# Searching one projection at a time, and U products 32 columns narrower, in a hybrid SSD/MLA block with a product-key expert mixer

## The chip, the cores and the metric

The kernel runs on one NeuronCore of a Trainium2 chip. TensorE (PE) multiplies, and its weight loads (PEld) overlap it; VectorE (DVE), ScalarE (ACT) and GpSimd (POOL) work beside it, and transfers are issued by queues of SyncE (SP), POOL and ACT. The metric is the device time of one execution in microseconds, the median of several runs.

## The reference

One decoder layer over 512 tokens of 1024 features, in float32. After a LayerNorm, an SSD part and an attention part are computed and mixed by one output projection, with a residual and a LayerNorm. Neither the change nor the stages it moves touch that part. Then comes the expert mixer:

```python
q = (xb @ w_query).reshape(T, PEER_HEADS, 2, PEER_HALF_DIM)          # 8 heads, 2 halves, 128
s = jnp.einsum('thkd,hknd->thkn', q, sub_keys).astype(jnp.float32)   # 128 sub-keys per half
sv, si = lax.top_k(s, K)                                             # K = 16
cand_s = (sv[:, :, 0, :, None] + sv[:, :, 1, None, :]).reshape(T, PEER_HEADS, K * K)
cand_i = (si[:, :, 0, :, None] * PEER_N_KEYS + si[:, :, 1, None, :]).reshape(T, PEER_HEADS, K * K)
top_s, top_pos = lax.top_k(cand_s, K)
expert_idx = jnp.take_along_axis(cand_i, top_pos, axis=-1)
gate = jax.nn.softmax(top_s, axis=-1)
u = jnp.take(u_table, expert_idx, axis=0)                            # 16384 experts x 1024
act = jax.nn.gelu(jnp.einsum('td,thkd->thk', xb, u).astype(jnp.float32), approximate=False)
v = jnp.take(v_table, expert_idx, axis=0)
return jnp.einsum('thk,thkd->td', (gate * act).astype(xb.dtype), v)
```

So each token chooses 128 of 16384 experts (8 heads x 16). The result gets a residual with factor ALPHA and a last LayerNorm.

## The kernel before, in words

The 512 tokens are four blocks of 128. Every float32 product is made of three products of rounded parts (`mm3`): high x high, high x low and low x high.

For blocks 0 to 2 (NT = 384 tokens) the mixer is dense. All 16384 experts are walked in 128 chunks of 128. A *U product* (`u_chunk`) multiplies a chunk of the U table with the 384 token columns, 8 x 3 matmuls, and ACT puts its GELU into an `act` tile. Gates are written into a dense matrix G: for each token, 128 one-hot pairs are multiplied on PE, so that G holds the gate at each chosen expert and zero elsewhere. A *V product* (`v_chunk`) takes P = act x G, splits it into a high part `Ph` (ACT) and a low part `Pl` (DVE), and multiplies it with a chunk of the V table into six accumulators `va`. Block 3 is not dense: for each of its 128 choices, an indirect DMA on POOL's queue fetches one U row per token, DVE forms the dot products, and later the V rows are added up (`gather`).

All big weights come through one stream (`Stream`, `items`). SP loads a raw tile (`wir`, 3 buffers), ACT rounds it to the high part (`wih`, in one place of four `wihx`), and DVE or POOL subtracts to make the low part (`wil`, line 115; 3 buffers). This subtraction is called a *split* here. A split of item n is issued with the use of item n - 2, waits until item n - 3 has been used, and is followed on SP by the load of a later item. `lo_on` says which engine splits: POOL during the search, DVE otherwise.

The order of the work is written by the program text, and each engine runs its list in order. The stages from about 412 us on:

1. Two U products, then 16 query projections (`w_query_fm`, each 24 matmuls of 512 columns), each followed by the scores of the projection before it against 128 sub-keys (four blocks, in PSUM banks that hold four projections each). Every fourth projection ACT copies the banks to `sc`.
2. The search on DVE (`stage1`, `top16`): for one block and four projections, the top 16 of 128 in two passes of 8, then 88 candidate sums (`cand`) for two heads and their top 16. It starts when four projections are scored.
3. The index stage on DVE (`stage2`): gates, and the expert's two 7-bit indices, block after block. `g_head` transposes the indices and gates of a block on PE.
4. The build (`build_g`): 48 groups of 8 tokens. For a group `hot` makes on DVE the one-hot tiles `oj` and `oi` (two compares) and the two gated tiles `g1` and `oi` (two products), in two buffers each. PE makes 16 fp16 matmuls, ACT copies them to a staging tile `stg`, and every fourth group SP stores 2 MB to a DRAM tensor `gsp`.
5. The second half: U products 54 to 127 alternate with V products 0 on, then V products alone. SP loads `gt` tiles back from `gsp`, which needs the last store. `gather` runs on POOL and DVE beside it.

U products of stages 2 to 4 are placed by a planner in the program text: `tm[0]` sums estimated PE time, `tm[1]` estimated DVE time (the generators yield estimates), and `drive` places a U product (`step_u`) whenever `tm[0] <= tm[1]`, while fewer than LEAD = 54 `act` tiles are filled. Left-over products up to 54 are put behind the build.

Of the kernel before, what the change touches and what calls it, by code (L numbers as in the profile page):

```python
# [11 lines left out]
F32 = mybir.dt.float32  # L12
# [12 lines left out]
D = 1024  # L25
# [5 lines left out]
NT = 384  # L31
LEAD = 54
LASTC = 120
T_U = 4.24
# [5 lines left out]
SCB = 10  # L40
# [9 lines left out]
def tile_block(ctx: ExitStack, tc: tile.TileContext, I, out):  # L50
# [140 lines left out]
    acd = dram.tile([64, 128], F32, name="acd")  # L191

# [676 lines left out]
    XTL = xt.tile([128, 8, S], F32R, name="XTL")  # L869
    lnq = pool("lnq", side="right")  # L870
# [34 lines left out]
    sc, scb, qT = {}, {}, {}  # L905

    def w_query_fm(m):
        if m < 16:
            h, l = item()
            h = h.rearrange("p (k c) -> p k c", k=8)  # L910
            l = l.rearrange("p (k c) -> p k c", k=8)
            ps = pw()
            for k in range(8):
                mm3(ps, h[:, k], l[:, k], XTH[:, k], XTL[:, k], k == 0, k == 7)
            qT[m] = rq.tile([128, S], F32, name="qT", bufs=2)
            A.activation(qT[m], ps, AF.Copy)
        if m > 0:
            m -= 1
            q = qT.pop(m)
            if m % 4 == 0 and m:  # L920
                load_sk(m // 4 + 1)
            for b in range(NB):
                if m % 4 == 0:
                    scb[b] = pu() if b >= 2 else px()
                T.matmul(scb[b][:, (m % 4) * 128:(m % 4 + 1) * 128], q[:, b * 128:(b + 1) * 128], SK[m // 4][:, m % 4],
                         start=True, stop=True)
                if m % 4 == 3:
                    t = rq.tile([128, 4, 128], F32, name="sc", bufs=SCB)
                    A.activation(t.rearrange("p a b -> p (a b)"), scb[b], AF.Copy)  # L929
                    for i in range(4):  # L930
                        sc[b, m - 3 + i] = t[:, i]

    TV, TI, TS, PO = {}, {}, {}, {}

    def top16(src, w, val, idx, gs):
        t2 = {}
        for g in gs:
            V.max(val[:, g, 0:8], src(g))
        for g in gs:
            V.max_index(idx[:, g, 0:8], val[:, g, 0:8], src(g))  # L940
        for g in gs:
            t2[g] = rt.tile([128, 128], F32, name="t2", bufs=4)[:, :w]
            V.match_replace(t2[g], val[:, g, 0:8], src(g), NEG)  # L943
        for g in gs:
            V.max(val[:, g, 8:16], t2[g])
        for g in gs:
            V.max_index(idx[:, g, 8:16], val[:, g, 8:16], t2[g])
        return len(gs) * (0.36 + w * 0.0064)
# [3 lines left out]
    def stage1(b, q):  # L952
        if q == 0:
            TV[b] = rt.tile([128, 16, 16], F32, name="tv", bufs=4)
            TI[b] = rt.tile([128, 16, 16], U32, name="ti", bufs=4)
            TS[b], PO[b] = TS4[:, b], PO4[:, b]
        yield top16(lambda g: sc[b, g], 128, TV[b], TI[b], range(4 * q, 4 * q + 4))
        tv = TV[b].rearrange("p (h e) a -> p h e a", e=2)[:, 2 * q:2 * q + 2]
        cand = rt.tile([128, 2, 88], F32, name="cand", bufs=3)
        for c0, a0, na, w in ((0, 0, 1, 16), (16, 1, 3, 8), (40, 4, 12, 4)):  # L960
            sh = [128, 2, na, w]
            V.tensor_tensor(cand[:, :, c0:c0 + na * w].rearrange("p h (a b) -> p h a b", a=na),
                            tv[:, :, 0, a0:a0 + na, None].to_broadcast(sh),
                            tv[:, :, 1, None, 0:w].to_broadcast(sh), op=OP.add)
        yield 0.5 + top16(lambda g: cand[:, g - 2 * q], 88, TS[b], PO[b], range(2 * q, 2 * q + 2))

    def stage2():
# [35 lines left out]
        for b in range(NB):  # L1003
            for c in range(2):
                A.activation(ti[:, b, :, :, :, c].rearrange("p e h a -> p h e a"),
                             TI[b].rearrange("p (h e) a -> p h e a", e=2), AF.Copy)
            eq = rt2.tile([128, 16, 16, 16], F16, name="eq")
            abv = abf[:, b].rearrange("p e (h k) -> p (e h) k", k=16)
            V.tensor_tensor(eq, abv[:, :, None, :].to_broadcast(sh), iaE[:, None].to_broadcast(sh), op=OP.is_equal)
# [3 lines left out]
            V.tensor_tensor(eqv, eqv, tv[:, :, None, :].to_broadcast([128, 256, 8, 2]), op=OP.mult)  # L1013
# [8 lines left out]
    GT = {}  # L1022

    def g_head(b):
# [4 lines left out]
        ijT = ijp.tile([128, 2, 128], F16, name="ijT", bufs=2)  # L1029
        gT = ijp.tile([128, 2, 128], F16, name="gT", bufs=2)  # L1030
        A.activation(ijT.rearrange("p a b -> p (a b)"), ps[:, 0:256], AF.Copy)
# [4 lines left out]
    def build_g():  # L1036
        bc = [128, 4, 128, 2]

        def hot(n):
# [3 lines left out]
            oj = gb.tile(bc, F16, name="oj", bufs=2)  # L1043
            oi = gb.tile(bc, F16, name="oi", bufs=2)
            g1 = gb.tile(bc, F16, name="g1", bufs=2)
            io = iotaE[:, None].to_broadcast(bc)
            V.tensor_tensor(oj, io, col(ijT[:, 1]), op=OP.is_equal)
            V.tensor_tensor(oi, io, col(ijT[:, 0]), op=OP.is_equal)
# [5 lines left out]
        step_u()  # L1054
        yield 2.7
        for n in range(48):
# [20 lines left out]
            yield 2.7 if n < 47 else 0.1  # L1077
# [39 lines left out]
    ap_ = pool("act")  # L1117
    ACT = {}

    def u_chunk(c, psum=None):  # L1120
# [18 lines left out]
    iaE = ijp.tile([128, 16, 16], F16, name="iaE")  # L1139
    nc.sync.dma_start(iotaE.rearrange("p a b -> p (a b)"), I["ch"][:, 0:256])  # L1140
    nc.sync.dma_start(iaE.rearrange("p a b -> p (a b)"), I["ch"][:, 256:512])
    rt = pool("rt", side="right")
    TS4 = rt.tile([128, NB, 8, 16], F32, name="ts")
    PO4 = rt.tile([128, NB, 8, 16], U32, name="po")
    rq = pool("rq")
# [32 lines left out]
    for m in range(17):  # L1178
        w_query_fm(m)
        tm[0] += T_Q  # L1180
        if m % 4 == 0 and m:
            fill = chain(fill, *[stage1(b, m // 4 - 1) for b in range(NB)])
            tm[1] = max(tm[1], tm[0])
# [7 lines left out]
    close(rq)  # L1191
    rt2 = pool("rt2")
    lo_on[0] = V
# [3 lines left out]
    gb = pool("gb", side="right")  # L1197
    drive(build_g())
# [34 lines left out]
    def v_sb(c, nm):  # L1233
        if c > LASTC:
            return ap_.tile([128, NT], F32, name="act", bufs=LEAD).bitcast(F32R)
# [139 lines left out]
    def ln_out(b):  # L1375
# [4 lines left out]
        for e in range(2):  # L1380
            V.scalar_tensor_tensor(t[:, ce[e]], t[:, ce[e]], ALPHA, va[b][e], op0=OP.mult, op1=OP.add)
# [22 lines left out]

    kept = sorted(held)
# [93 lines left out]
```

## Time and profile before

| | |
|---|---|
| median of 3 runs | 1666.66 us (1665.42 to 1666.8) |
| the profiled execution | 1663.19 us |
| its span | 1661.2 us |
| mean granted PE clock | 0.995 |
| busy: PE, DVE, ACT, POOL | 97%, 82%, 41%, 27% of the span |
| DMA | 384.80 MB, mean 232 GB/s |
| start of the search, index stage, first group on DVE | 455.84, 575.19, 627.29 us |
| last group's DVE work ends, first V product starts | 792.20, 816.18 us |

A row of the order of time has its start, its duration, engine, line and operation, what it writes and reads, the shape, and in brackets how long the engine had been idle and what ended that. Matmul durations overlap, so the pace of PE is read from the starts. A window's row has the stretch, the busy time of PE, PEld, DVE, ACT and POOL with counts, the granted clock, the DMA share and GB/s. L115 is a helper's line (the split).

### The profile page before, as it was taken

To read this page: it belongs to the slowest core of one execution; us is meant where nothing else is said; L and a number is where in the kernel's file an instruction comes from. 1 tells how busy PE (TensorE), PEld (TensorE's weight loads), DVE (VectorE), ACT (ScalarE), POOL (GpSimd) and SP (SyncE) were. 2 spreads that over 40 slices of the span, in tenths; PEclk is the share of its full clock that TensorE was granted. 3 is DMA by queue.
4 is the path that set the end of the run, shared out by engine and by line. 5 is a ranking of instruction groups with operands and counts; after the bars stand their busy time and mean duration, and the time that the engine had idled before them with its cause. 6 is when DMAs were issued, how large, how long until landed. Compare 5 with 4: busy or idle time off the path is not lost.

```text
span 1661.2 us, 23589 instructions
## 1 busy us (share of the span) xinstructions
PE 1618.6 (97%) x8639; PEld 1426.9 (86%) x8639; DVE 1358.3 (82%) x2673; ACT 685.4 (41%) x1082; POOL 449.2 (27%) x315
## 2 busy tenths in 40 slices
PE   7999999999999999999999999999999999999997
PEld 5878777888888998999999999999999999888886
DVE  8979688947299998999487878778788888998977
ACT  5574466632333344555333333333333333333331
POOL 0000000000334400000144555545454544543300
PEclk9999999999999999999999999999999999999999
DMA  6242111463332335666699999999899999999973
GB/s 240 97 151 84 56 54 57 128 237 123 121 98 82 115 125 174 234 237 246 225 364 337 339 319 331 337 333 322 319 342 334 331 320 340 348 344 339 337 227 119
DMA packets 146211, 384.80 MB, mean 232 GB/s; under 512 B 11936, under 2 KB 62368, under 8 KB 144304
## 3 DMA queue, kind: packets, MB, share of 16 engines
q1 hardware_dynamic: 105536, 237.24, 41.4%
q0 software_dynamic: 40416, 145.80, 24.2%
q8 instruction: 67, 1.10, 0.3%
q14 instruction: 48, 0.39, 0.1%
q10 hardware_dynamic: 144, 0.26, 0.0%
HBM read 350.72 MB, written 31.49 MB: 230 GB/s over the span
## 4 chain that ended last, share of the span: by engine, by line
PE 77%; DVE 19%; issue 2%; ACT 1%; DMA 1%; DVEq 0%; SPq 0%; ACTq 0%
PE va L1256 11%; PE va L1257 11%; PE va L1260 11%; PE pu L68 8%; PE pu L70 8%; PE pu L69 8%; PE pa L68 3%; PE pa L70 3%; PE pa L69 3%; DVE wil L115 2%; DVE g L1049 1%; PE pw L69 1%; PE pw L70 1%; PE pw L68 1%; DVE t L943 1%
## 5 line engine op out<-in xcount | busy, mean ns | idle before, releaser
L115 DVE TENSOR_TENSOR wil<-wir,wih 128x1024 fp32r<-128x1024 f32 (+1 forms) x249 | 295.9, 1189 | 116.6 <-issue 59.5
L105 ACT ACTIVATE wih<-wir 128x1024 fp32r<-128x1024 f32 (+2 forms) x269 | 277.7, 1033 | 220.5 <-DMA wir<-v 85.0
L70 PE MATMUL pu<-XTH,wil 128*128 128x384 f32 x1008 | 341.9, 339 | 0.0
L68 PE MATMUL pu<-XTH,wih 128*128 128x384 f32 x904 | 309.2, 342 | 1.0 <-ACT sc L929 1.0
L69 PE MATMUL pu<-XTL,wih 128*128 128x384 f32 x904 | 306.5, 339 | 0.0
L1293 POOL DMA_INDIRECT row<-u,ix x128 | 187.1, 1462 | 425.9 <-DVE g L1278 252.3
L1257 PE MATMUL va<-wil,Ph 128*128 128x512 f32 x726 | 283.6, 391 | 0.0
L1293 POOL DMA_INDIRECT row<-v,ix x128 | 182.3, 1424 | 204.3 <-DVE ac L1310 174.5
L1128 ACT ACTIVATE act<-pu 128x384 f32<-128x384 f32 x126 | 61.9, 491 | 317.4 <-PE pu L70 317.3
L70 PEld LDWEIGHTS pu<-XTH,wil 128*128 128x128 f32 x1008 | 189.7, 188 | 0.0
L68 PEld LDWEIGHTS pu<-XTH,wih 128*128 128x128 f32 x904 | 170.3, 188 | 4.0 <-ACT sc L929 1.2
L69 PEld LDWEIGHTS pu<-XTL,wih 128*128 128x128 f32 x904 | 170.5, 189 | 2.8
L1256 PE MATMUL va<-wih,Ph 128*128 128x512 f32 x432 | 168.5, 390 | 0.0
L1310 DVE SCALAR_TENSOR_TENSOR ac<-row,hd,ac 128x1024 f32<-128x1024 f32 x128 | 164.0, 1281 | 2.7 <-DMA row<-v,ix 0.5
L1257 PEld LDWEIGHTS va<-wil,Ph 128*128 128x128 f32 x726 | 136.2, 188 | 26.4
L1304 DVE SCALAR_TENSOR_TENSOR row<-row,x 128x1024 f32<-128x1024 f32 x128 | 150.0, 1219 | 2.1 <-DMA row<-u,ix 2.0
L1260 PE MATMUL va<-wih,Pl 128*128 128x512 f32 x432 | 133.3, 390 | 0.0
L105 ACT ACTIVATE wihx<-wir 128x1024 fp32r<-128x1024 f32 x67 | 71.2, 1063 | 145.2 <-DMA wir<-v 101.2
L115 DVE TENSOR_TENSOR wil<-wir,wihx 128x1024 fp32r<-128x1024 f32 x61 | 74.6, 1222 | 60.5 <-issue 55.5
L1256 PE MATMUL va<-wihx,Ph 128*128 128x512 f32 x294 | 115.0, 391 | 1.5 <-ACT Ph L1240 1.5
L115 POOL TENSOR_TENSOR wil<-wir,wih 128x1024 fp32r<-128x1024 f32 x20 | 49.5, 2474 | 193.7 <-PE pw L70 165.8
L1260 PEld LDWEIGHTS va<-wih,Pl 128*128 128x128 f32 x432 | 81.1, 188 | 16.9
(435 smaller groups left out, 3062.9 us busy)
## 6 DMA issues: line engine op xcount, KB each, us to landing
wir<-ut SPq DMA_DIRECT2D x128, 512.0 KB, 5.2
wir<-v SPq DMA_DIRECT2D x128, 512.0 KB, 6.4
gsp<-stg SPq DMA_DIRECT2D x12, 2048.0 KB, 7.2
gt<-gsp SPq DMA_DIRECT2D x32, 768.0 KB, 10.0
wir<-wo SPq DMA_DIRECT2D x26, 512.0 KB, 3.8
wir<-wf SPq DMA_DIRECT2D x18, 512.0 KB, 3.3
wir<-wqr SPq DMA_DIRECT2D x16, 512.0 KB, 3.6
de<-acd POOLq DMA_DIRECT2D x8, 512.0 KB, 5.2
```

What stands on the lines that cost most here:

```text
L68: T.matmul(ps, lh, rh, start=start, stop=False)
L69: T.matmul(ps, lh, rl, start=False, stop=False)
L70: T.matmul(ps, ll, rh, start=False, stop=stop)
L105: A.activation(h, r, AF.Copy)
L115: self.lo(n).tensor_tensor(l, r, h, op=OP.subtract)
L1128: A.activation(ACT[c], ps, AF.Gelu)
L1256: T.matmul(va[b][e], Ph[:, bs], h[:, cs], start=c == 0, stop=False)
L1257: T.matmul(va[b][e], Ph[:, bs], l[:, cs], start=False, stop=False)
L1260: T.matmul(va[b][e], Pl[:, bs], h[:, cs], start=False, stop=c == 127)
L1293: G.indirect_dma_start(out=R[s], out_offset=None, in_=I["u"] if s < 128 else I["v"], in_offset=bass.IndirectOffsetOnAxis(ap=ix[:, s % 128: ...
L1304: V.scalar_tensor_tensor(r, r, 1.0, x3, op0=OP.mult, op1=OP.mult, accum_out=hd[:, s:s + 1])
L1310: V.scalar_tensor_tensor(ac, r, hd[:, s - 128:s - 127], ac, op0=OP.mult, op1=OP.add)
```

## The change

**The search goes projection by projection.** The scores of a projection now stand inside the next one, after its third of eight k steps, in one PSUM bank for all four blocks, and are copied out at once. `stage1(m)` searches one projection for four blocks; after every second one come the candidates of one head for four blocks. `TV4` and `TI4` hold the results of all blocks.

**U products have 352 columns.** NU = NT - 32: the last 32 tokens of block 2 are left out of the products. Their 32 columns of each `act` tile are filled with ones (`one`, an ACT copy).

**These 32 tokens get their activations by gathering.** The index stage takes block 2 first, and `ug_index` writes their 32 x 128 expert indices to DRAM and reads them back with 4 choices x 32 tokens on the 128 partitions, on POOL's queue; the gates go the same way. 32 indirect DMAs (`ug_fetch`, two buffers) each fetch 128 U rows, and in build groups 1 to 32 DVE makes one dot product each (`ug_dots`), followed by a GELU and another trip over DRAM. `ug_head`, after group 41, multiplies activation and gate, scales each token by its largest magnitude, transposes, and puts the product into the gate tile of block 2. Since `act` is one there, P is right; `scl` multiplies the scale back in the last addition of block 2 (`ln_out`), whose residual ACT has multiplied by ALPHA before.

**The build.** The two compares of a group are one, over both indices (`ij`); `ijT` is laid out for that.

**The planner.** T_U is 3.9, a group 2.55. The row buffers lie where 8 of the 54 `act` tiles go (`KEEP = 46`): until the dots are done and the pool `ug` is closed, only 46 U products may be placed. In the engines' lists as they come out, PE has 21 U products between the last projection and the first group, 23 one by one between the first groups, none between groups 23 and 33, eight in a row behind group 33, and none between the last 14 groups; one stands before the first V product. DVE has the eight splits of that row ahead of the compare of group 35. 21 splits are POOL's (before: 26). The table `iaE` is loaded later, into `rt2`.

```diff
@@ scores inside the next projection
+        for k in range(8):
+            if m < 16:
                 mm3(ps, h[:, k], l[:, k], XTH[:, k], XTL[:, k], k == 0, k == 7)
+            if k == 2 and m > 0:
+                sub_scores(m - 1)
...
+    def sub_scores(m):
+        q = qT.pop(m)
+        if m % 4 == 0 and m:
+            load_sk(m // 4 + 1)
+        ps = px()
+        for b in range(NB):
+            bs = slice(b * 128, (b + 1) * 128)
+            T.matmul(ps[:, bs], q[:, bs], SK[m // 4][:, m % 4], start=True, stop=True)
+        sc[m] = rq.tile([128, NB, 128], F32, name="sc", bufs=SCB)
+        A.activation(sc[m].rearrange("p a b -> p (a b)"), ps, AF.Copy)
...
+    def stage1(m):
+        yield top16(sc.pop(m), 128, TV4[:, :, m], TI4[:, :, m])
+        if m % 2:
+            h = m // 2
...
+            yield 0.7 + top16(cand, 88, TS4[:, :, h], PO4[:, :, h])
@@ index stage
-        for b in range(NB):
+        for b in (2, 0, 1, 3):
...
             if b == 2:
+                ug_index(p3)
+            if b == 1:
                 g_head(0)
@@ gathered vectors
+    def ug_fetch(n):
+        if n < UG:
+            UR[n] = ug.tile([128, D], F32, name="urow", bufs=2)
+            G.indirect_dma_start(out=UR[n], out_offset=None, in_=I["u"],
+                                 in_offset=bass.IndirectOffsetOnAxis(ap=UR["ix"][:, n:n + 1], axis=0))
+
+    def ug_dots():
+        for n in range(UG):
+            r = UR.pop(n)
+            V.scalar_tensor_tensor(r, r, 1.0, UR["x"], op0=OP.mult, op1=OP.mult, accum_out=UR["hd"][:, n:n + 1])
+            ug_fetch(n + 2)
+            yield 1.2
...
+        close(ug)
+        aps.append(pool("act2"))
+        yield 0.1
+
+    def ug_head():
+        w, g = UR["w"], UR["g"]
+        mx, r = UR["m"][:, 0:1], UR["m"][:, 1:2]
+        V.tensor_tensor(w, w, g, op=OP.mult)
+        V.scalar_tensor_tensor(g, w, -1.0, w, op0=OP.mult, op1=OP.max)
+        V.tensor_reduce(mx, g, axis=AX.X, op=OP.max)
...
+        T.transpose(ps[:, :UG], w, ident[:UG, :UG])
...
@@ build
-            V.tensor_tensor(oj, io, col(ijT[:, 1]), op=OP.is_equal)
-            V.tensor_tensor(oi, io, col(ijT[:, 0]), op=OP.is_equal)
+            V.tensor_tensor(ij.rearrange("p e q i c -> p (e q) i c"), iotaE[:, None].to_broadcast(b2),
+                            ijT[:, n % 16].rearrange("p e (q c) -> p (e q) c", c=2)[:, :, None, :].to_broadcast(b2),
+                            op=OP.is_equal)
+            oi, oj = ij[:, 0], ij[:, 1]
...
+            if n >= 1:
+                tm[1] += next(dots, 0.0)
+            if n == 41:
+                ug_head()
+                tm[1] += 1.2
-            yield 2.7 if n < 47 else 0.1
+            yield 2.55 if n < 47 else 0.1
@@ U products
-        ps = (psum or pu)()[:, :NT]
+        ps = (psum or pu)()[:, :NU]
         for k in range(8):
-            mm3(ps, h[:, k], l[:, k], XTH[:, k, :NT], XTL[:, k, :NT], k == 0, k == 7)
-        ACT[c] = ap_.tile([128, NT], F32, name="act", bufs=LEAD)
-        A.activation(ACT[c], ps, AF.Gelu)
+            mm3(ps, h[:, k], l[:, k], XTH[:, k, :NU], XTL[:, k, :NU], k == 0, k == 7)
+        ACT[c] = act_tile()
+        A.activation(ACT[c][:, NU:], one, AF.Copy)
+        A.activation(ACT[c][:, :NU], ps, AF.Gelu)
@@ planner
-            if tm[0] <= tm[1] and un[0] < LEAD:
+            if tm[0] <= tm[1] and un[0] < (LEAD if len(aps) > 1 else KEEP):
@@ last addition
+            if b == 2:
+                V.scalar_tensor_tensor(t[:, ce[e]], va[b][e], scl, t[:, ce[e]], op0=OP.mult, op1=OP.add)
...
+    A.activation(xr[2], xr[2], AF.Copy, scale=ALPHA)
```

More of the change, by code (lines that the diff above doesn't have):

```diff
@@ L31 @@
 NT = 384
+UG = 32
+NU = NT - UG
 LEAD = 54
+KEEP = 46
 LASTC = 120
-T_U = 4.24
+T_U = 3.9
 T_Q = 6.3
@@ new lines, in top16 @@
+    def top16(src, w, val, idx):
+        t2 = []
+        for b in range(NB):
+            V.max(val[:, b, 0:8], src[:, b])
+        for b in range(NB):
+            V.max_index(idx[:, b, 0:8], val[:, b, 0:8], src[:, b])
+        for b in range(NB):
+            t2.append(rt.tile([128, 128], F32, name="t2", bufs=4)[:, :w])
+            V.match_replace(t2[b], val[:, b, 0:8], src[:, b], NEG)
+        for b in range(NB):
+            V.max(val[:, b, 8:16], t2[b])
+        for b in range(NB):
+            V.max_index(idx[:, b, 8:16], val[:, b, 8:16], t2[b])
+        return NB * (0.36 + w * 0.0064)
@@ L1053, in build_g @@
         nxt = hot(0)
-        step_u()
-        yield 2.7
+        dots = ug_dots()
+        tm[1] += 3.0
+        yield 2.6
         for n in range(48):
@@ L1180, in tile_block @@
         tm[0] += T_Q
-        if m % 4 == 0 and m:
-            fill = chain(fill, *[stage1(b, m // 4 - 1) for b in range(NB)])
-            tm[1] = max(tm[1], tm[0])
+        if m:
+            fill = chain(fill, stage1(m - 1))
+            tm[1] = max(tm[1], tm[0] - 3.0)
         while tm[1] < tm[0] + T_Q:
```

127 lines of the change are left out of this document (68 added, 59 removed).

## The prediction

> **What bounds the kernel now.** I read the page first, then stages of 100 us, then the order of time on TensorE (PE) and VectorE (DVE) from the search to the second half.
>
> ```profile
> PE 1618.6 (97%) x8639; PEld 1426.9 (86%) x8639; DVE 1358.3 (82%) x2673; ACT 685.4 (41%) x1082; POOL 449.2 (27%) x315
> ...
> PE 77%; DVE 19%; issue 2%; ACT 1%; DMA 1%; DVEq 0%; SPq 0%; ACTq 0%
> ```
>
> The chain that ended last is PE with a fifth of DVE. The stages tell where that fifth lies (columns: stretch, busy time by engine, granted clock, DMA share, GB/s).
>
> ```profile
> 600.00:700.00 100.00, 94.12 (x727) 91.14 (x726) 93.01 (x120) 49.52 (x83) 0.00 (x0) 0.97 0.52 179
> 900.00:1000.00 100.00, 100.00 (x504) 91.12 (x503) 79.83 (x118) 35.17 (x48) 52.67 (x35) 1.00 0.94 327
> 1400.00:1500.00 100.00, 100.00 (x460) 85.17 (x459) 87.91 (x101) 36.00 (x49) 48.71 (x33) 1.00 0.97 343
> ```
>
> From about 816 us on (U and V products) PE never stops; DVE is the pace from the search (456 us) to the end of the build (792 us), with PE filled by U products beside it.
>
> **What a narrower U product is worth.** Starts of a U product, of the V product behind it, and of 256-wide products:
>
> ```profile
> 1004.36 0.34 PE L68 MATMUL pu<-XTH,wih 128*128 128x384 f32 x1
> 1008.60 0.40 PE L1256 MATMUL va<-wih,Ph 128*128 128x512 f32 x1
> ...
> 214.34 0.28 PE L69 MATMUL pu<-wil,kvh 128*128 128x256 f32 x1
> 215.53 0.28 PE L70 MATMUL pu<-wih,kvl 128*128 128x256 f32 x1
> ```
>
> 24 matmuls take 4.24 us, 0.1767 us each. Ten 256-wide ones start within 1.19 us, 0.119 each. On the line between, 352 columns cost 0.1623 us: 3.894 us a product, 0.346 less. 55 of the 128 products lie before the first V product, 73 behind it. There nothing hides PE, so 73 x 0.346 = **25.3 us** go. The new 32-wide ACT copy per product lies on an engine busy 35 of 100 us there: nothing; without that cover, 128 short copies.
>
> **The search starts earlier.**
>
> ```profile
> 423.08 0.49 PE L68 MATMUL pw<-XTH,wih 128*128 128x512 f32 x1 [0.25 <-ACT XTH L902]
> 434.98 0.60 PE L925 MATMUL px<-SK,qT 128*128 128x128 f32 x4
> 441.47 0.61 PE L925 MATMUL px<-SK,qT 128*128 128x128 f32 x4
> ...
> 455.84 0.87 DVE L938 MAX8 tv<-sc 128x8 f32<-128x128 f32 x4 [31.39 <-ACT sc L929]
> 462.97 0.85 DVE L938 MAX8 tv<-sc 128x8 f32<-128x128 f32 x4
> 467.64 0.46 DVE L962 TENSOR_TENSOR cand<-tv 128x32 f32<-128x32 f32 x3
> 470.07 0.85 DVE L938 MAX8 tv<-sc 128x8 f32<-128x128 f32 x4
> 575.19 0.67 DVE L972 TENSOR_TENSOR dd<-ts 128x512 f32<-128x512 f32 x1
> ```
>
> Now DVE waits 31 us for four score groups, 6.49 us apart. After the change the first scores stand 9 matmuls into the second projection. Projections begin 0.6 us earlier (two narrower U products), at 422.5; one projection with its start is about 6.3 us, nine matmuls 2.1: scores at 430.9, and, with 1.8 us for four products and the copy out, search from 432.7. One score group costs 467.64 - 462.97 = 4.67 us; the candidates of two heads 470.07 - 467.64 = 2.43, of four blocks about 4.45 (the additions rise less than twofold). 16 x 4.67 + 8 x 4.45 = 110.3; 1.8 us of waiting for the second group; today's 119.35 us exceeds 16 x 7.10 by 5.7 (bounds 0 to 5.7), of which I keep 2.6. The search ends at **547.4**, 27.8 us earlier.
>
> **Index stage and build.**
>
> ```profile
> 586.69 2.28 DVE L1009 TENSOR_TENSOR eq<-abf,iaE 128x4096 f16<-128x4096 f16 x1
> 588.89 1.21 DVE L115 TENSOR_TENSOR wil<-wir,wih 128x1024 fp32r<-128x1024 f32 x1
> 590.03 2.28 DVE L1013 TENSOR_TENSOR eq<-eq,tif 128x4096 f16<-128x4096 f16 x1
> ...
> 627.29 0.69 DVE L1047 TENSOR_TENSOR oj<-iotaE,ijT 128x1024 f16<-128x1024 f16 x1
> 633.74 0.68 DVE L1047 TENSOR_TENSOR oj<-iotaE,ijT 128x1024 f16<-128x1024 f16 x1
> 634.35 0.68 DVE L1048 TENSOR_TENSOR oi<-iotaE,ijT 128x1024 f16<-128x1024 f16 x1
> 635.06 0.69 DVE L1049 TENSOR_TENSOR g<-oi,gT 128x1024 f16<-128x1024 f16 x1
> 636.40 0.68 DVE L1047 TENSOR_TENSOR oj<-iotaE,ijT 128x1024 f16<-128x1024 f16 x1
> ...
> 1002.78 1.22 DVE L1304 SCALAR_TENSOR_TENSOR row<-row,x 128x1024 f32<-128x1024 f32 x1
> 1003.93 1.22 DVE L1304 SCALAR_TENSOR_TENSOR row<-row,x 128x1024 f32<-128x1024 f32 x1
> ```
>
> The index stage took 627.29 - 575.19 = 52.1 us. One more split of a weight (590.03 - 588.89 = 1.14), the index arithmetic (0.3) and a wait for the PE transposes of the first block, now late (1.6), make 55.1: first group's DVE work at 602.5. The x rows and the small table queue on SP behind loads that U products of the search need, not ahead of them; the index round trip over DRAM is on POOL's queue with some 35 us to spare: nothing.
>
> A group costs DVE 2.66 us. Its two compares (1.32) become one of twice the size: between 0.61 and 2.20 for 1024 and 4096 elements lies 1.14, plus the 0.1 of a dependent successor, 1.25; a group 2.59 (bounds 2.45 to 2.7). A dot with a gathered row adds 1.15, a split 1.14. The group of PE:
>
> ```profile
> 778.16 0.23 PE L1067 MATMUL pw<-oi,oj 128*128 128x128 f16 x1
> 779.98 0.42 PE L68 MATMUL pu<-XTH,wih 128*128 128x384 f32 x1
> 784.30 0.23 PE L1067 MATMUL pw<-oi,oj 128*128 128x128 f16 x1
> ...
> 802.05 1.23 DVE L115 TENSOR_TENSOR wil<-wir,wih 128x1024 fp32r<-128x1024 f32 x1 [3.02 <-PE pu L70]
> ```
>
> Two groups take 1.82 us, 0.91 each; a narrower product there 4.32 - 0.35 = 3.97. So group and product cost PE 4.88 and group, dot and split cost DVE 4.88. Projections end at 527, 21 products and the transposes at 609.2; with DVE's third group this meets at 613. Then, in DVE's new order, 32 groups with a dot, 22 of them with a split: 32 x 3.74 + 22 x 1.14 = 144.8; 1 for two gate tiles; 2 for the coupling (the build's 164.9 us from 627.29 to 792.2 hold 6.7 beyond its 48 x 2.66, 26 splits and gate tiles, so 0 to 6.7); and 3 for rows that land late (below). DVE is done with group 34 at **763.8**. In the last ten of these PE has 0.91 us of work in 3.74: the limit of 46 products holds it idle.
>
> Then eight products stand in a row on PE, and eight splits on DVE ahead of group 35. The row at 802.05 shows what a split does there: three buffers, so it waits until the product three places back is through. DVE is held for the whole run. PE begins it after group 33, 761.8, runs 8 x 3.89 + 2.5 (clock), and is through at 795.4, group 34 at 796.3. Twelve groups at 2.59 without any product beside them and 3 us for the gathered gates (six small operations, a transpose, a copy; 1.5 to 6) end at **830.4**.
>
> **The hand-over.**
>
> ```profile
> 792.20 1.22 DVE L115 TENSOR_TENSOR wil<-wir,wih 128x1024 fp32r<-128x1024 f32 x1
> ...
> 794.12 0.33 SPq L1074 DMA_DIRECT2D gsp<-stg  x1
> 808.31 1.35 SPq L1215 DMA_DIRECT2D gt<-gsp  x2
> ...
> gsp<-stg SPq DMA_DIRECT2D x1, 2048.0 KB, 7.3
> ...
> 814.97 0.56 DVE L1227 TENSOR_TENSOR P<-act,gt 128x384 f32<-128x384 f32 x1 [7.45 <-DMA gt<-gsp]
> ...
> 816.18 0.51 PE L1256 MATMUL va<-wihx,Ph 128*128 128x512 f32 x1 [1.51 <-ACT Ph L1240]
> ```
>
> 1.9 us to the store's issue, 7.3 to land, 6.7 for the load back (today issued late, behind weight loads on SP's queue), 1.2 to the first V product: 17.1. Five U products cover it today; one is left. First V product at 847.5 against 816.18: **+31.3**, and 2 for a cold clock.
>
> ```profile
> 636.00:637.00 1.00, 0.46 (x5) 0.50 0.00 0
> ```
>
> The clock fell to 0.50 here after two gaps of 1.6 us with 0.9 us of work between; half speed for up to 5.9 us would cost 0 to 2.95 in either place. I take 2.5 and 2. The Trainium skill (TensorE: Matmul & The Clock Gate, What's actually happening) has the clock halve only after an idle window of about 3.4 us. By that rule the gaps before the run of eight would not halve it, and the sum would be 2.5 us lower; this case's row disagrees, and the row decides.
>
> **Sum:** 31.3 + 2 - 25.3 = +8.0 us. The scaled last addition and one early ACT copy change nothing at the end. The profiled execution took 1663.19 us, 1671.2 after; the median is 3.5 above it: **1674.7**. Differences under 0.2% (3.3 us) cannot be told from none.
>
> **Rivals.**
>
> Not slower: the hand-over is short. These are the GB/s from 785 to 810 us, in 40 slices.
>
> ```profile
> GB/s 419 210 210 85 360 360 59 0 7 301 360 164 7 0 0 210 472 393 367 498 446 446 157 367 33 269 413 420 419 125 52 321 354 138 0 0 0 72 111 295
> ```
>
> Single slices reach 446 and more. With empty queues the store's 2 MB may land in 4.6 us and the load in half of 6.7. Price 6.1, time 1668.6; it decides from 4.7. Against it: today's store had little beside it.
>
> The group is cheaper: a fused compare that cost no more than one of today (0.71 with its successor's wait) takes 0.54 from the 21 groups with no product beside them, 11.3 us: 1663.4, faster if it is less still. Against it: compares grow with their size in the rows above.
>
> Warm clock: PE's gaps before the run of eight are 3.74 - 0.91 = 2.8 us; if they do not slow it, 2.5 us less, 1672.2.
>
> Late rows: only two row buffers. A row must land within two groups less a dot and a hand-shake (1.35): 8.4 us with products, 6.1 without.
>
> ```profile
> DMA to landing us min/median/max: 5.6/8.5/11.0
> ```
>
> At 8.5 the ten groups without products lose 12 us, 9 more than I took: 1684; at 11 all 32 lose, over 50. [...]
>
> Memory is the limit in the second half: 327 GB/s must become 341 for the whole gain. The stage at 343 with PE full speaks against it; half the gain lost is 1687. And the change may not do what it says: a matmul that does not get shorter below 384 columns gives 44 us back, about 1719; the 256-wide rows speak against it.
>
> **Chances.** Forecast 0.46; short hand-over 0.15; warm clock 0.08; cheap group or a build otherwise shorter 0.13; late rows 0.10; memory 0.06; width 0.02. Cheap group makes faster, 0.13; short hand-over and 0.02 of the forecast's low end the same, 0.17; the rest, 0.70, slower. The range takes 1660 to 1688; the forecast's own is 1670 to 1682.
>
> **What would show it.** Search from about 433 to 547 us; 0.162 us between 352-wide matmuls; group 35's compare some 25 us behind its predecessor with splits waiting on PE between; thirteen groups with PE mostly idle; first V product 27 to 35 us later than now; from there to the end about 25 us less. Wrong, if the first V product comes by 841 us, or dots wait for rows, or PE waits in the second half.

## The result, and the profile after

The changed kernel takes 1685.8 us (median of four runs, 1685.18 to 1688.45), the kernel before 1666.34 in the runs beside it (1665.42 to 1666.8). The ratio is 1.012, interval 1.0104 to 1.0135: 19.5 us slower, where 8 were forecast. The profiled execution took 1685.18 us, its span is 1683.4.

The page of the changed kernel, busy times and the chain that ended last:

```profile
PE 1594.6 (95%) x8640; PEld 1399.9 (83%) x8640; DVE 1397.7 (83%) x2680; ACT 704.0 (42%) x1213; POOL 495.5 (29%) x349
...
PE 81%; DVE 8%; issue 6%; POOL 2%; DMA 2%; ACT 2%; DVEq 0%; POOLq 0%; ACTq 0%; SPq 0%
```

TensorE (PE) does 24 us less work than before, and VectorE (DVE) 39 more. POOL is new on the chain with 2%, and DMA's share of it goes from 1% to 2%. The stages, in the columns of the prediction's second fence:

```profile
600.00:700.00 100.00, 94.51 (x739) 92.13 (x738) 89.68 (x110) 49.94 (x95) 25.22 (x15) 0.97 0.71 250
700.00:800.00 100.00, 74.41 (x562) 70.81 (x562) 77.79 (x99) 38.57 (x73) 26.56 (x17) 0.78 0.68 245
800.00:900.00 100.00, 78.95 (x507) 71.55 (x507) 65.34 (x89) 36.13 (x64) 17.54 (x13) 0.78 0.64 230
900.00:1000.00 100.00, 100.00 (x528) 90.61 (x527) 83.70 (x124) 37.98 (x62) 53.32 (x36) 1.00 0.97 352
1400.00:1500.00 100.00, 100.00 (x486) 86.75 (x485) 89.71 (x97) 38.07 (x57) 51.61 (x35) 1.00 0.99 358
```

From 900 us on PE is full, as before, and the DMA engines deliver 352 and 358 GB/s where they delivered 327 and 343. From 700 to 900 us PE and DVE are both idle for a fifth to a third of the time: neither is the limit there, waits between them are. DVE's instructions give the milestones (columns: start, duration, engine and line, tiles; in brackets the idle time ahead and what ended it):

```profile
437.30 0.87 DVE L946 MAX8 tv<-sc 128x8 f32<-128x128 f32 x4 [10.14 <-ACT sc L941]
552.83 0.67 DVE L977 TENSOR_TENSOR dd<-ts 128x512 f32<-128x512 f32 x1
607.16 1.22 DVE L1102 TENSOR_TENSOR ij<-iotaE,ijT 128x2048 f16<-128x2048 f16 x1
...
782.37 1.23 DVE L1052 SCALAR_TENSOR_TENSOR urow<-urow,ux 128x1024 f32<-128x1024 f32 x1 [3.48 <-DMA urow<-u,uix]
...
783.52 1.22 DVE L1102 TENSOR_TENSOR ij<-iotaE,ijT 128x2048 f16<-128x2048 f16 x1
...
802.01 1.23 DVE L118 TENSOR_TENSOR wil<-wir,wih 128x1024 fp32r<-128x1024 f32 x1 [2.61 <-PE pu L73]
...
810.83 1.22 DVE L1102 TENSOR_TENSOR ij<-iotaE,ijT 128x2048 f16<-128x2048 f16 x1
...
814.41 1.23 DVE L1102 TENSOR_TENSOR ij<-iotaE,ijT 128x2048 f16<-128x2048 f16 x1 [0.91 <-PE pw L1126]
817.00 1.22 DVE L1102 TENSOR_TENSOR ij<-iotaE,ijT 128x2048 f16<-128x2048 f16 x1
...
845.18 1.22 DVE L1102 TENSOR_TENSOR ij<-iotaE,ijT 128x2048 f16<-128x2048 f16 x1
...
862.70 0.56 DVE L1308 TENSOR_TENSOR P<-act,gt 128x384 f32<-128x384 f32 x1 [14.85 <-DMA gt<-gsp]
```

The search runs from 437.30 to 552.83, the first group starts at 607.16. The last dot starts at 782.37, the compare of group 34 (groups are counted from 0) 1.15 us later at 783.52, so that group is done at 783.52 + 2.59 = 786.1. Then the splits of the row of eight products wait for PE, up to the compare of group 35 at 810.83; that of group 36, at 814.41, waits 0.91 us more for PE. From there groups follow each other in 2.59; the last ends at 845.18 + 2.59 = 847.8. The first V product is this row of PE:

```profile
863.87 0.80 PE L1337 MATMUL va<-wihx,Ph 128*128 128x512 f32 x1 [8.64 <-ACT Ph L1321]
```

| stretch, us | forecast | measured | difference |
|---|---|---|---|
| start to search | 432.7 | 437.3 | +4.6 |
| search | 114.7 | 115.5 | +0.8 |
| index stage, to the first group | 55.1 | 54.3 | -0.8 |
| first group to group 34 done | 161.3 | 178.9 | **+17.6** |
| from there to the last group | 66.6 | 61.7 | -4.9 |
| hand-over, to the first V product | 17.1 | 16.1 | -1.0 |
| first V product to the end of the span | 821.7 | 819.5 | -2.2 |

The differences add up to 14.1, and 1685.18 - 1671.2 is 14.0. One stretch holds more than all of it, the groups with dots. The 4.9 us that come back behind it belong to it for the larger part: while the last dot waited 3.48 us for its row, PE had already begun the row of eight (at 780.59, which is 5.5 us before group 34 was done; the forecast had 2.0). The group of the dots in the list of costly instructions, its busy time and mean, and the idle time ahead of it with its releaser:

```profile
L1052 DVE SCALAR_TENSOR_TENSOR urow<-urow,ux 128x1024 f32<-128x1024 f32 x32 | 39.0, 1220 | 22.2 <-DMA urow<-u,uix 22.2
```

DVE waited 22.2 us for gathered rows; the forecast had 3. There are eight waits. Three of them, then SP's stores of finished blocks in the same stretch:

```profile
639.94 1.23 DVE L1052 SCALAR_TENSOR_TENSOR urow<-urow,ux 128x1024 f32<-128x1024 f32 x1 [2.06 <-DMA urow<-u,uix]
661.27 1.23 DVE L1052 SCALAR_TENSOR_TENSOR urow<-urow,ux 128x1024 f32<-128x1024 f32 x1 [1.75 <-DMA urow<-u,uix]
680.21 1.22 DVE L1052 SCALAR_TENSOR_TENSOR urow<-urow,ux 128x1024 f32<-128x1024 f32 x1 [5.18 <-DMA urow<-u,uix]
```

```profile
630.09 0.33 SPq L1132 DMA_DIRECT2D gsp<-stg  x1
649.43 0.33 SPq L1132 DMA_DIRECT2D gsp<-stg  x1
668.92 0.42 SPq L1132 DMA_DIRECT2D gsp<-stg  x1
```

Each of the eight comes about ten microseconds behind the issue of a 2 MB store (639.94 behind 630.09, 661.27 behind 649.43, 680.21 behind 668.92), once in a block of four groups. That raises the question for the experiments: do rows come late because of the store, or are two buffers too few for what a fetch takes anyway, or is GpSimd (POOL) held up when it issues the fetches?

### The profile page after: what moved, and what is told of

It reads as the page before. It is cut to its first block, busy times and chain, and to the rows that moved or that the text cites. A ratio compares the mean times of both kernels' runs of the same rounds, so it can differ in the third digit from the quotient of the medians.

```text
span 1683.4 us, 23810 instructions
## 1 busy us (share of the span) xinstructions
PE 1594.6 (95%) x8640; PEld 1399.9 (83%) x8640; DVE 1397.7 (83%) x2680; ACT 704.0 (42%) x1213; POOL 495.5 (29%) x349
## 4 chain that ended last, share of the span: by engine, by line
PE 81%; DVE 8%; issue 6%; POOL 2%; DMA 2%; ACT 2%; DVEq 0%; POOLq 0%; ACTq 0%; SPq 0%
PE va L1337 10%; PE va L1338 10%; PE va L1341 10%; PE pu L71 9%; PE pu L72 9%; PE pu L73 9%; PE pa L73 3%; PE pa L72 3%; PE pa L71 3%; PE pw L72 3%; PE pw L73 3%; PE pw L71 3%; POOL urow L1046 2%; DVE ij L1102 1%; PE pb L490 1%
## 5 line engine op out<-in xcount | busy, mean ns | idle before, releaser
L118 DVE TENSOR_TENSOR wil<-wir,wih 128x1024 fp32r<-128x1024 f32 (+1 forms) x253 | 300.9, 1190 | 109.3 <-ACT wih L108 58.9
L73 PE MATMUL pu<-XTH,wil 128*128 128x352 f32 x1008 | 327.4, 325 | 0.0
L71 PE MATMUL pu<-XTH,wih 128*128 128x352 f32 x904 | 296.5, 328 | 0.0
L72 PE MATMUL pu<-XTL,wih 128*128 128x352 f32 x904 | 294.6, 326 | 0.0
L1198 ACT ACTIVATE act<-pu 128x352 f32<-128x352 f32 x126 | 58.4, 464 | 188.6 <-PE pu L73 188.4
L118 DVE TENSOR_TENSOR wil<-wir,wihx 128x1024 fp32r<-128x1024 f32 x62 | 78.0, 1259 | 43.0 <-issue 32.7
L1125 PE MATMUL pw<-ij 128*128 128x128 f16 x384 | 64.6, 256 | 41.3 <-DVE ij L1107 41.3
```

Source lines behind the costliest of these rows:

```text
L71: T.matmul(ps, lh, rh, start=start, stop=False)
L72: T.matmul(ps, lh, rl, start=False, stop=False)
L73: T.matmul(ps, ll, rh, start=False, stop=stop)
L118: self.lo(n).tensor_tensor(l, r, h, op=OP.subtract)
L1125: T.matmul(ps[:, t * 128:(t + 1) * 128], oj[:, q, :, c], oi[:, q, :, c], start=True, stop=False)
```

## Experiments

### What makes the rows late: the store twice, and in quarters

```
             if g % 4 == 3:
                 nc.sync.dma_start(gsp[b * 4 + g // 4], stg)
+                if n < 32:
+                    nc.sync.dma_start(gs2[b * 4 + g // 4], stg)
```

> Each of the first eight stores of the build is issued twice, the second time to another place in memory; nothing reads the copy. Theory A (rows queue behind stores): the waits for rows about double, 35 to 55 us, the time 1698 to 1720. Theory B (latency or GpSimd): waits stay near 22 us, the time within 4 us of 1686. If the staging buffers come free too late, ACT waits for them, which would show as a wait on stg and not on urow.

```
+        full = []
...
-            if g % 4 == 3:
-                nc.sync.dma_start(gsp[b * 4 + g // 4], stg)
+            if g % 4 == 3:
+                full.append((b * 4 + g // 4, stg))
+            k, s4 = full[-1] if full else (0, None)
+            if n == 47:
+                nc.sync.dma_start(gsp[k], s4)
+            elif n >= 3:
+                cs4 = slice((n + 1) % 4 * 32, (n + 1) % 4 * 32 + 32)
+                nc.sync.dma_start(gsp[k][:, cs4], s4[:, cs4])
```

> The 2 MB store of a finished block of the build is cut into four stores of 512 KB, one behind each of the next four groups; the last block's goes out whole. Theory A (a gathered row queues behind the store's packets on the shared DMA engines): the 22.2 us that dots wait for rows fall under 10, group 34 comes 12 to 18 us earlier, the time is 1668 to 1674. Theory B (two row buffers are too few for the plain latency, or GpSimd is kept from writing descriptors): the waits stay at 18 to 26 us, the time within 4 us of 1686.

The store twice: 1702.2 us (ratio 1.0209, interval 1.0192 to 1.0226). The store in quarters: 1674.5 us (1.0047, 1.0030 to 1.0064). Dots and fetches of the doubled store, of the changed kernel, and of the quarters (the same view of three kernels; the dot's row of the changed kernel stands above):

```profile
L1047 POOL DMA_INDIRECT urow<-u,uix x32 | 53.6, 1675 | 156.5 <-DVE urow L1053 153.4 <-DMA uix<-ugi 2.8 <-issue 0.3
L1053 DVE SCALAR_TENSOR_TENSOR urow<-urow,ux 128x1024 f32<-128x1024 f32 x32 | 39.1, 1221 | 41.6 <-DMA urow<-u,uix 41.6
```

```profile
L1046 POOL DMA_INDIRECT urow<-u,uix x32 | 53.4, 1669 | 139.7 <-DVE urow L1052 136.4 <-DMA uix<-ugi 3.0 <-issue 0.3
```

```profile
L1046 POOL DMA_INDIRECT urow<-u,uix x32 | 53.5, 1672 | 130.5 <-DVE urow L1052 127.4 <-DMA uix<-ugi 2.8 <-issue 0.3
L1052 DVE SCALAR_TENSOR_TENSOR urow<-urow,ux 128x1024 f32<-128x1024 f32 x32 | 39.1, 1222 | 10.1 <-DMA urow<-u,uix 10.1
```

The waits go 41.6, 22.2, 10.1 us with nothing changed but the stores, and the times follow them. Against the kernel before, timed beside each, the three take 35.0, 19.5 and 7.3 us more: +15.6 and -12.2 us, where +19.4 and -12.1 us of waiting were added and taken. (The quarters are at the edge of what theory A gave, 10.1 us for "under 10" and 1674.5 for 1668 to 1674.) In the doubled run ACT never waits for a staging buffer. What POOL spends on a fetch stays at 1.67 to 1.68 us in all three, so whatever POOL meets there is no cause of the differences. Theory B falls as the cause of these differences: it is the store that makes the rows late. The 10.1 us that are left with quarters, in 16 short waits, no run explains. How the store does it (rows behind its packets, as theory A has it, or both waiting on memory) these runs do not tell. The Trainium skill (DMA: Bandwidth & Descriptors, Issuing engines are not separate DMA queues) says that transfers started by SP and by GpSimd run on the same DMA engines and interleave; the three waits (41.6, 22.2 and 10.1 us) agree with it.

### What the waits cost: three row buffers

```
-KEEP = 46
+KEEP = 43
...
-            UR[n] = ug.tile([128, D], F32, name="urow", bufs=2)
+            UR[n] = ug.tile([128, D], F32, name="urow", bufs=3)
...
-            ug_fetch(n + 2)
+            ug_fetch(n + 3)
```

> Three buffers for gathered rows instead of two, each row fetched three groups ahead; for their space eleven products instead of eight are held back to the end of the dots. By both theories on the rows (behind stores, or latency) the waits fall from 22.2 to 0 to 5 us: this prices them. Against it three more products in the row, 3 x 3.9 us of PE behind the dots, less 3 splits of 1.14 ahead: +8. Time 1686 - 20 + 8 = 1674, range 1669 to 1680. If the waits were covered by something else, 1690 to 1694.

Measured 1671.7 us (1.0029, 1.0019 to 1.0038), within the range. No dot waited:

```profile
L1052 DVE SCALAR_TENSOR_TENSOR urow<-urow,ux 128x1024 f32<-128x1024 f32 x32 | 38.9, 1217 | 0.0
```

Of the 22.2 us some 14 reach the time (1685.8 less 1671.7). The rest goes against the row of products, now eleven long, and against the 3.48 us that the last dot had waited beside it. The stretch to the end of the dots, which no longer waits on anything but DVE, is also a clean look at the clock: PE's longest gap there is 2.64 us, and from 713 us on the gaps are 1.20 to 2.64 us. Two starts of a group on PE, and then stages of this kernel:

```profile
717.13 0.29 PE L1125 MATMUL pw<-ij 128*128 128x128 f16 x1 [2.64 <-DVE ij L1107]
720.86 0.29 PE L1125 MATMUL pw<-ij 128*128 128x128 f16 x1 [1.85 <-DVE ij L1107]
```

```profile
710.00:715.00 5.00, 2.10 (x33) 1.75 (x32) 4.93 (x7) 2.48 (x5) 1.81 (x2) 0.96 0.98 389
715.00:720.00 5.00, 1.89 (x16) 1.62 (x16) 4.90 (x7) 1.34 (x3) 2.94 (x2) 0.50 0.56 199
...
750.00:755.00 5.00, 2.23 (x20) 1.98 (x21) 4.90 (x8) 1.19 (x2) 0.00 (x0) 0.50 0.98 416
```

The granted clock falls to 0.50 with such gaps and stays there for 40 us.

### The row of eight products

```
-            if tm[0] <= tm[1] and un[0] < (LEAD if len(aps) > 1 else KEEP):
+            if tm[0] <= tm[1] and un[0] < KEEP + rel[0]:
...
+            if n in (35, 38, 41, 44):
+                rel[0] += 1
```

> The eight U products held back until the dots are through no longer stand in a row: one is let go behind each of groups 35, 38, 41 and 44, and four stand behind the last group. Theory C (the row holds DVE, as its splits wait for buffers, and the hand-over is uncovered): from group 34's end at 786 us the rest takes 13 x 2.59 + 4 x 1.2 + 2.3 = 41 us, last group at 827 instead of 847.8; the hand-over then takes 16 to 22 us, as the load queues behind weights on SP; first V product at 843 to 849 instead of 863.9, the time 1665 to 1671. Rival (PE has this work to do in any case and only moves it): within 4 us of 1686.

Measured 1677.1 us (1.0052, 1.0034 to 1.0069): theory C is right in sign, 8.7 us instead of 15 to 21. DVE after the dots (rows of DVE in order of time):

```profile
796.76 1.23 DVE L1102 TENSOR_TENSOR ij<-iotaE,ijT 128x2048 f16<-128x2048 f16 x1 [2.42 <-PE pw L1126]
...
820.90 1.22 DVE L1102 TENSOR_TENSOR ij<-iotaE,ijT 128x2048 f16<-128x2048 f16 x1 [2.60 <-PE pw L1126]
...
831.14 1.23 DVE L1102 TENSOR_TENSOR ij<-iotaE,ijT 128x2048 f16<-128x2048 f16 x1 [1.26 <-PE pw L1126]
...
856.30 0.56 DVE L1311 TENSOR_TENSOR P<-act,gt 128x384 f32<-128x384 f32 x1 [6.89 <-DMA gt<-gsp]
```

Two things ate the rest. A product of 3.9 us on PE between groups of 2.59 on DVE holds back the group behind it, so that a compare waits 1.26 to 2.6 us (the compares' buffers are two), and the last group ends at 831.14 + 2.59 = 833.7, not 827. And with four weight loads ahead of it on SP's queue the gate load is late: from there to the first V product (857.52) it is 23.8 us, where the changed kernel took 16.1. So the last group comes 14 of the forecast 21 us earlier, and the later hand-over takes 8 of these back. The rival's number (within 4 us of 1686) does not hold either; that part of the row was PE work which has to be done in any case fits the result, but no run separates it.

### The width alone

```
-        ps = (psum or pu)()[:, :NT]
+        ps = (psum or pu)()[:, :NU]
...
-        A.activation(ACT[c], ps, AF.Gelu)
+        A.activation(ACT[c][:, NU:], one, AF.Copy)
+        A.activation(ACT[c][:, :NU], ps, AF.Gelu)
```

> The kernel before with nothing changed but the width: U products 352 columns wide, and ones in the place of the 32 other inputs, whose vectors are left out of the computation. My term: 73 x 0.346 = 25.3 us less from the first V product to the end. Ahead of it DVE is the pace, but PE stood at 93 to 98% there: 0 to 13 us more. Time 1628 to 1641. If memory limits the second half: half of it, 1652 to 1656 and a DMA rate that stays near 340 GB/s with PE waiting.

Measured 1635.1 us (0.9806, 0.9789 to 0.9822). Its span is 1634.3, and its first V product is this:

```profile
816.52 0.50 PE L1260 MATMUL va<-wihx,Ph 128*128 128x512 f32 x1 [2.03 <-ACT Ph L1244]
```

So from the first V product to the end it takes 817.8 us, 27.2 less than before (forecast 25.3). The first V product itself comes no earlier (816.52 against 816.18), although PE had less to do ahead of it. One reason may be the start of the search: it is 4.6 us later in this run (460.47 against 455.84; see the late start below), and no run has the width alone without that. In this order of the work the narrower products bring 27 us, and the gather has to be cheaper.

### The search without the gather

```
-UG = 32
-NU = NT - UG
+NU = NT
...
-KEEP = 46
+KEEP = LEAD
...
-T_U = 3.9
+T_U = 3.7
```

and all that has `ug` or `UR` in its name taken out.

> The change without the gather: search by projection and the fused compare stay, U products are 384 wide, no rows, no dots, no held products, the end as before; 3.7 us planned for a product, so that five are left behind the last group as in the kernel before. If DVE alone were the limit, the search (20 us) and the 48 groups (0.07 us each) would bring the first V product to about 793 and the time to 1643. Theory: PE stood idle for only 11 of the 396 us from 420 to 816 in the kernel before, so no more than that can go: first V product at 806 to 814, time 1656 to 1664. If the search gives nothing, 1667.

Measured 1654.8 us (0.9929, 0.9911 to 0.9946), 1.2 us below the range; the first V product, at 806.61, is within it. The stretch from 420 to 816 us of the kernel before and of this one:

```profile
420.00:816.00 396.00, 384.83 (x2581) 359.04 (x2579) 333.84 (x1102) 169.27 (x269) 64.03 (x26) 0.99 0.48 166
```

```profile
420.00:816.00 396.00, 390.32 (x2626) 363.93 (x2626) 340.95 (x1047) 174.41 (x276) 57.06 (x24) 1.00 0.50 169
```

PE was busy for 384.8 of 396 us already, so a search that ends 26 us earlier on DVE (549.01 against 575.19) brings the first V product 9.6 us forward and no more. This part of the change is a gain by itself. The gather, with the row of held products and the hand-over left uncovered, turns it into a loss: the first V product comes at 863.87 instead of 806.61, 57 us later, of which the narrower products give 25.5 back, and some 31 remain between the two kernels.

### The late start of the search

Ahead of the search, DVE's splits and the one of POOL in the changed kernel:

```profile
421.45 1.22 DVE L118 TENSOR_TENSOR wil<-wir,wih 128x1024 fp32r<-128x1024 f32 x1
422.59 3.38 DVE L118 TENSOR_TENSOR wil<-wir,wihx 128x1024 fp32r<-128x1024 f32 x1
425.89 1.27 DVE L913 TENSOR_TENSOR XTL<-px,XTH 128x512 fp32r<-128x512 f32 x2
```

```profile
421.87 3.01 POOL L118 TENSOR_TENSOR wil<-wir,wih 128x1024 fp32r<-128x1024 f32 x1 [128.14 <-PE pw L73]
```

In the kernel before, the same two splits began in the other order:

```profile
422.03 1.22 DVE L115 TENSOR_TENSOR wil<-wir,wihx 128x1024 fp32r<-128x1024 f32 x1
```

```profile
422.10 3.40 POOL L115 TENSOR_TENSOR wil<-wir,wih 128x1024 fp32r<-128x1024 f32 x1 [129.60 <-PE pw L70]
```

A split of this size takes 1.22 us on DVE and, begun 0.72 us behind a split on POOL, 3.38. The order goes with the width of the products ahead: in the run with the width alone DVE's split takes 3.37 us, in the run without the gather, at full width, 1.22. Two runs tried to part them; the first asks for POOL's split one projection later, the second gives it to DVE.

```
     lo_on[0] = G
+    win.la = 1
...
         w_query_fm(m)
+        win.la = 2
```

> GpSimd's first split of a query weight is asked for one projection later, so that it cannot run beside VectorE's split ahead of the last XTL. If the two engines keep each other out there (VectorE's split 3.38 us instead of 1.22, TensorE idle and its clock lowered behind it), the split takes 1.22, the search starts at 433 to 434 instead of 437.3 and the time is 1681 to 1683. If the late start is TensorE's own, the search starts at 437 as before and the time stays at 1686.

```
-    lo_on[0] = G
...
         w_query_fm(m)
+        lo_on[0] = G
```

> VectorE instead of GpSimd does the split of a query weight that ran beside the split ahead of the last XTL. Here the two cannot meet: the split ahead of XTL should take 1.22 us instead of 3.38, and the span from its start to the first score search should fall from 14.7 us (422.59 to 437.30) to 12.5; the time from 1685 to about 1683. If the 3.38 us are not from the meeting, both stay. A change of 2 us of the time can hardly be told; the durations can.

The first gave 1683.7 us (1.0093, 1.0074 to 1.0113) and tests nothing: POOL has no other work there, so its split started (420.26) 0.73 us ahead of DVE's as before, and DVE's took 3.38 us again. The second, 1680.2 us (1.0100, 1.0071 to 1.0129), parts them; here are its rows of DVE:

```profile
421.19 1.22 DVE L118 TENSOR_TENSOR wil<-wir,wihx 128x1024 fp32r<-128x1024 f32 x1
...
432.35 0.88 DVE L946 MAX8 tv<-sc 128x8 f32<-128x128 f32 x4 [7.61 <-ACT sc L941]
```

The split takes 1.22 us, and from its start to the first search it is 11.2 us instead of 14.7: 3.5 us of the late start go with this meeting. In the time the difference cannot be told apart (the intervals overlap). The Trainium skill (SBUF — State Buffer, SBUF: two separate sides) describes a pair of ports that GpSimd shares with DVE: a DVE operation with two SBUF inputs and a GpSimd operation that reads SBUF exclude each other, and whoever starts first has the pair for the whole instruction. The trace agrees: POOL's split in the changed kernel ends at 421.87 + 3.01 = 424.88, and 1.1 us later DVE's is through.

### All repairs, and half the gather

Three row buffers, stores in quarters, the edit of the first split run, the products let go one by one, and two gate loads issued ahead of the weights of the last four, with 32 gathered inputs:

```
+            if n in (33, 34, 36, 38, 40, 42, 44):
+                rel[0] += 1
...
+    close(gb)
+    gtp = pool("gtp")
+    load_g(0)
+    load_g(1)
     uc = un[0]
     while uc < LEAD:
```

> All repairs together: stores in quarters, three row buffers, GpSimd's first split one projection later, held products let go one by one (seven beside groups 33 to 44, four behind the last), and the first two loads of gates issued ahead of the weights of those four. From the first V product at 863.9: rows -20, row of products -18, late start -3, gate load -5: 818, time 1640, range 1632 to 1652. If the repairs overlap (the same idle time counted twice), 1655 to 1668.

Measured 1648.85 us (0.9888, 0.9871 to 0.9905): 1.1% faster than the kernel before, within the range, and 9 us above its middle. The first V product came at 831.1 instead of 818. The 3 us of the late start were not won (the search starts at 437.19), as the edit of the first split run parts nothing. One mishap is visible on DVE:

```profile
825.13 1.23 DVE L118 TENSOR_TENSOR wil<-wir,wihx 128x1024 fp32r<-128x1024 f32 x1 [9.49 <-ACT wihx L108]
```

The gate load, put ahead of the weights on SP's queue, waits there for the last store to land, and the weights behind it wait too. Then the same with 16 gathered inputs instead of 32, and the first query split on DVE:

```
-UG = 32
+UG = 16
...
+            if 18 <= n < 14 + LEAD - KEEP:
+                rel[0] += 1
```

> Only 16 inputs by gathered vectors (16 fetches, 16 dots, products 368 wide), with three row buffers, stores in quarters, the first query split on VectorE, held products let go one by one from group 18 and four of them behind the last group, gate loads ahead of their weights. VectorE from the first group at 607: 48 x 2.59 + 16 x 1.22 + 27 splits x 1.14 + 2.3 for the gathered gates = 177, last group at 784; four products and the load behind it, first V product at 803; from there 845 less half of the 27.2 us that 352 columns brought: 831. Time 1636, range 1630 to 1645. If the balance of the two engines is not what decides, it comes no lower than the 1648.9 of all repairs with 32 inputs.

Measured 1639.9 us (0.9853, 0.9826 to 0.9879), in the range; the first V product came at 811.80, later than 803, and the rest took 826.4, less than 831. Two stages of its build:

```profile
607.00:690.00 83.00, 83.00 (x671) 80.69 (x671) 80.06 (x99) 44.13 (x86) 22.39 (x13) 1.00 0.80 269
690.00:740.00 50.00, 48.62 (x433) 46.60 (x432) 47.56 (x56) 28.64 (x57) 1.22 (x2) 1.00 0.74 249
```

PE and DVE are both busy for 95% and more up to 740 us, where 32 dots left PE idle from 710 us on (busy for 2.10 of 5 us in the run with three row buffers), and no dot waits. From the run of all repairs this one differs in more than the 16 inputs (the first query split, the groups at which products are let go), so the gain between the two is not the balance alone. Last, the gate loads behind two of the weight loads:

```
     while uc < LEAD:
+        if uc == LEAD - 2:
+            load_g(0)
+            load_g(1)
```

> As the run with 16 gathered inputs, but the first two gate loads are issued behind the weight loads of the first two left-over products instead of ahead of all. There SP stood behind the last store for 6.4 us (790.47 to 796.88) with the weights queued behind it, and the last split waited 7.02 us for them. If that wait sets the first V product (811.8), it comes 4 to 7 us earlier, at 805 to 808, the ratio to the kernel before goes from 0.985 to 0.981 to 0.983. If the landing of the gates sets it, nothing changes.

Measured 1638.4 us (0.9829, 0.9816 to 0.9842). The wait of 7.02 us is gone, the last split comes at 801.08 instead of 807.22, but the first V product is at 808.83, just behind the 805 to 808 that were expected: 3.0 us earlier, of which 1.7 because the groups started 1.7 us earlier in this run. PE's own products now end there; the wait was mostly hidden by them. The interval overlaps with that of the run before it. Of the kernels that leave nothing out of the computation this one has the lowest ratio, 1.7% faster than the kernel before, with the search by projection and half of the gather.

## Why the prediction was right and wrong

**The step that failed** is the term of the build, "3 for rows that land late". It measured 22.2 us. The rival "late rows" had the place right and the condition wrong: it took one landing time for every row, the 8.5 us of fetches in the second half of the kernel before, and so put the loss into the ten groups without products. In the trace 13.4 us of the waits lie in groups with products and 8.8 behind them; that the rival's 1684 comes near the measured 1685.8 is luck. What decided is what else is being moved at the time: a 2 MB store once in four groups, on another queue. The diff did not touch these stores, and I read their line only for the hand-over. The prediction's own sign of being wrong, that dots wait for rows, came true; and the first V product came 47.7 us later than in the kernel before, where 27 to 35 were given.

**The second error** is the start of the search, 4.6 us late. 3.5 of it go with the split that met POOL's. POOL's split waits for a U product to release its buffer (the releaser in its row). In the kernel before it began at 422.10, 0.07 us behind DVE's at 422.03, and POOL waited; with two narrower products ahead it came 0.8 us earlier against DVE's, and the order turned round. I had taken this stretch as a plain shift.

**Right:** the search (115.5 against 114.7) and index stage (54.3 against 55.1); the group at 2.59 us to the digit, and a dot at its 1.15; the run of eight that holds DVE (group 35's compare at 810.83, 27 us behind its predecessor, 25 forecast); the hand-over (16.1 against 17.1); the clock before the run: 0.50 there, 14 matmuls at 0.29 us apart instead of 0.16 cost 1.8 us, 2.5 forecast, so "warm clock" falls. The gathered gates took 2.3 us, 3 forecast. The term of the second half, 25.3 us, came whole: 25.5 in the changed kernel (845.0 - 819.5), which holds the cold clock too (granted 0.50 from 863 to 870 us; 2 us forecast), and 27.2 with the width alone, where PE had products up to the first V product. The memory rival falls, as 352 to 358 GB/s were there, and "width no gain" with it. "Cheap group" and "short hand-over" fall by the rows above.

**The sign** stands on the ground that the prediction gave: the first V product comes later by more than the second half wins. The row of held products and the uncovered hand-over did that even without the waits for rows: with three row buffers no dot waits, and the kernel is still 4.7 us slower than the kernel before (1.0029, 1.0019 to 1.0038), with eleven products in the row. What I had not seen is that half the gather fits into the time that the search sets free on DVE, and then both engines are nearly full through most of the build.

**Open:** whether rows queue behind the store in the DMA engines or wait on memory; the DMA engines' busy share there (0.98 from 710 to 715 us in the run with three row buffers) does not tell these apart.

## What to carry to other kernels

A transfer that a tight loop waits for has to be timed with everything else on the DMA engines beside it, from any queue: look for the largest store in the same stretch, cut it up, or give the loop one buffer more. When two engines are both nearly full, a change that moves work between them gains only up to the point where they are even, so size it before arranging it (here 16 inputs did better than 32, though the two kernels differ in other edits too). Asking for an instruction later in the program holds nothing back on an engine that has no other work; only a dependence or another engine does.

## What the runs showed of the hardware

- The clock was halved in a stretch without a long gap: in the run with three row buffers PE's gaps were 1.20 to 2.64 us, with 1.1 to 2.5 us of work between them, and the granted clock stood at 0.50 from 715 to 755 us. The Trainium skill (TensorE: Matmul & The Clock Gate, What's actually happening) asks for an idle window of about 3.4 us; these rows have none, and they decide.
- Two splits of 128x1024 that take 1.22 us on DVE and 2.4 on POOL (433.78 in the changed kernel) took 3.38 and 3.0 when POOL's began 0.72 us ahead of DVE's, and 0.42 us behind an earlier one of DVE (421.45).
- A fetch of 128 rows of 4 KB held POOL for 1.67 us on average in all three kernels whose dots waited 41.6, 22.2 and 10.1 us, so that POOL's time says nothing on when data arrive.
